# Three of four MLP passes: when the weights of the way down are loaded

## The chip, the core and the metric

The kernel runs on one core of a Trainium2 chip. The core's engines work side by side, each on its own queue of instructions in order: TensorE (PE in the profile) multiplies matrices into PSUM, VectorE (DVE) and ScalarE (ACT) work on elements, GpSimd (POOL) does some of the sums here, and SyncE (SP) issues nearly all DMAs. The metric is the device time of one execution in microseconds; lower is better.

## The reference

One layer of a decoder trunk on 1024 tokens of width 1024, all in float32: a gated linear attention with its residual, then an MLP with its residual, then a last RMSNorm. The change concerns the MLP alone:

```python
def sqrelu_mlp(h, w1, w2):
    return jnp.square(jax.nn.relu(h @ w1)) @ w2
...
        x = x + mixers[i % N_MIXERS](rms_norm(x, norm_mix), *mix_params)
        x = x + sqrelu_mlp(rms_norm(x, norm_ffn), w1, w2)
    return rms_norm(x, final_norm)
```

`w1` is 1024 x 4096 and `w2` is 4096 x 1024.

## The kernel before

**Products.** A 1024 x 1024 x 1024 product is cut into blocks of 512 ("11", "12", "21", "22") and done in seven steps by a Winograd scheme instead of eight. `form` (L147) says for each side which block or which sum of blocks a step uses; a temporary "t" holds sums. In each step the 512-blocks are multiplied by `step` (L232): four lanes of 128 rows by four k-tiles by three matmuls (`mm3`, L72), since each float32 operand is split into a rounded high part and a rest (`split`, L79: the high part on ScalarE, L81, the rest on VectorE, L82). So a step is 48 matmuls of 128 x 512. The order of the steps is 0, 5, 1, 2, 3, 4, 6 on the way up and 0 to 6 on the way down.

**Passes.** The hidden width of 4096 is handled in four chunks of 1024. The plan (L1104 to L1108) is a list: entry 0 is the attention's output product; then for each chunk c an up pass (entry 1 + 2c: `w1` columns times x, into `hd[c]`, with square and ReLU) and a down pass (entry 2 + 2c: `hd[c]` times `w2` rows, added onto y). `chunks_of` (L262) walks the plan. At step `at` it takes the operands that are ready, may load weights for the next entry, makes the operands of the next step (`operand`, L266: sums, then splits), and emits the matmuls of this step.

**The x side.** The up pass of chunk 0 makes its seven forms of x on VectorE and ScalarE (`xside`) and stores each one, split, to DRAM (`xw`, 1 MB in each of two halves). The up passes of chunks 1 to 3 have the side `Stored` (L1024): no sums and no splits, only two 1 MB loads from `xw` a step (L1034), into tiles "big". There are 8 such tiles, four to a step's operands, so a form's load waits until TensorE has finished the step before last of its use.

**The weight side.** `weight_side` (L214) loads blocks into tiles "wa" (6) and "wb" (4) in two halves of 0.5 MB. The tags (L211) cross over: the up pass has 11 and 21 in "wa", 22 and 12 in "wb"; the down pass has 11 and 21 in "wb", 12 and 22 in "wa"; both have "t" in "wa". So the loads for a down pass take the buffers of the up pass before it as these come free. The sums of the weight side run on POOL (L184), except in the up pass of chunk 0, where VectorE does them. The first two sums of a down pass are t = 12 - 11 and 12 = 22 - 12, each in two halves: four POOL operations.

**What sets the order.** TensorE's order is written by hand (`manual_schedule`). The other engines' order is laid out by the tile framework's planner at compile time: of the instructions whose inputs and buffers it reckons ready, the one earliest in the program goes first. It may so put a load several steps ahead of where the program names it. `order_after(..., wait=False)` (L41) adds an edge that only the planner obeys: this instruction is placed behind that one. At run time each queue is served in order, and a DMA whose buffer is not free holds up all that SyncE has behind it.

**The place of the change.** In `chunks_of` the weights of the next entry are loaded at `at == 5` (for a down pass 11, 12 and 22: six loads) and at `at == 6` (21: two loads). Where the present entry has stored x (entries 3, 5, 7), these loads come behind `operand(*nxt)` in the program, and in `from_down` (L924) each carries an edge to `last["xw"]`, the latest load of a stored form. At `at == 5` that is the last form of the pass. Other edges to `last["xw"]` (L980, L992, L1056) belong to the turning of x in DRAM, and stay.

Of the kernel before, what the change touches and what calls it, by code (L numbers as in the profile page):

```python
# [40 lines left out]
def order_after(tc, inst, other, wait=True):  # L41

    kind = mybir.DependencyClass.Sync if wait else mybir.DependencyClass.NoSync
    tc.add_manual_dep(inst.ins, other.ins.name, mybir.DependencyInfo(kind, mybir.DependencyReason.DATA),
                      reason="order of phases")
# [3 lines left out]
def hybrid_trunk(ctx: ExitStack, tc: tile.TileContext, x, xT, w_head, w_r, w_gk, w_up,  # L49
                 w_out, w_ff1, w_ff2, vecs, g_fin, out):  # L50
    nc = tc.nc
# [25 lines left out]
    last = {}  # L77
# [41 lines left out]
    def run(general):  # L119
# [8 lines left out]
        def half(hf):  # L128
            return slice(hf * 512, hf * 512 + 512)
# [102 lines left out]
        def step(n, lhs, rhs, sink, by_lane=False, between={}, fine=False):  # L232

            b = BANK[n]

            def product(lane, kp):
                kh, k = kp // 2, kp % 2
                if n in (0, 1, 5) and kp == 0:
                    bank[b, lane] = new("gl" if b == "U" or lane == 0 else "mm")
                ls = slice(lane * P, lane * P + P)  # L240
                mm3(bank[b, lane], lhs[kh][:, k, 0, ls], lhs[kh][:, k, 1, ls], rhs[kh][:, k, 0, :], rhs[kh][:, k, 1, :],
                    n in (0, 1, 5) and kp == 0, n in (3, 5, 6) and kp == 3, True)
                if kp == 3:
                    sink(n, lane, bank[b, lane])

            if by_lane:
                for lane in range(4):
                    for kp in range(4):
                        product(lane, kp)
                        for f in between.get((lane, kp), ()):  # L250
                            f()
            elif fine:
                for kp in range(4):
                    for lane in range(4):
                        product(lane, kp)
            else:
                for kh in range(2):
                    for lane in range(4):
                        product(lane, 2 * kh)
                        product(lane, 2 * kh + 1)  # L260

        def chunks_of(plan, ops, hooks, sinks, last_by_lane=False, turns={}):  # L262

            def operand(i, at):  # L266

                which, order = plan[i][2], plan[i][4]
                w, x_ = plan[i][which], plan[i][1 - which]
                made = {}  # L270
                for turn in turns.get((i, at), ("W", "n", "x", "X") if which == 0 else ("x", "X", "W", "n")):
                    if callable(turn):
                        turn()
                    elif turn == "x":
                        x_.sums(order[at])
                    elif turn == "X":
                        made[1 - which] = x_.split(order[at])
                    elif turn == "w":
                        w.sums(order[at])
                    elif turn == "W":  # L280
                        made[which] = w.split(order[at])
                    elif at + 1 < len(order):
                        w.sums(order[at + 1])
                return made[0], made[1]

            def load(i, names):
                if i < len(plan):
                    w = plan[i][plan[i][2]]
                    for name in names[w.s_form]:
                        w.load(name)  # L290

            if not ops:
                ops.append(operand(0, 0))
            for i, (_, _, _, sink, order) in enumerate(plan):
                for at, n in enumerate(order):
                    for f in hooks.get((i, at), ()):
                        f()
                    cur = ops.pop(0)
                    stored = getattr(plan[i][1], "stored", False)
                    loads = {5: {True: ("11", "12"), False: ("11", "12", "22")}, 6: {True: ("21", "22"), False: ("21",)}}.get(at)  # L300
                    if loads and not stored:
                        load(i + 1, loads)
                    nxt = (i, at + 1) if at + 1 < len(order) else (i + 1, 0)
                    if nxt[0] < len(plan):
                        ops.append(operand(*nxt))
                    if loads and stored:
                        load(i + 1, loads)
                    for f in hooks.get((i, at, "then"), ()):
                        f()
                    here = {k[2:]: v for k, v in hooks.items() if len(k) == 4 and k[:2] == (i, at)}  # L310
                    final_step = last_by_lane and (i, at) == (len(plan) - 1, 6)
                    step(n, *cur, sinks.get((i, at), sink), bool(here) or final_step, here, (i, at) in fine_steps)
# [176 lines left out]
        class KeptX:  # L489

            s_form = False
# [358 lines left out]
        if not general:  # L850
# [10 lines left out]
                          (2, 0, 3, 3): (g(prep_fast, 2, 1),), (2, 3, "then"): (g(prep_fast, 3, 1),),  # L861
                          (2, 4, 2, 1): (g(operands, 0, "mm"),)})
        chunks_of([(wqk, xq, 0, qk_into, PLAIN), (xk, wv, 1, v_into, PLAIN), (xr_, wR, 1, r_into, R_FIRST)], ops_a, hooks, {},
                  turns={(0, 1): ("X", split_gate, "W"), (0, 2): ("x", "X", "w", "W", lambda: last.update(sums=last["split"], s1=last["sum"], s1_low=last["low"]), "n"),
                         (0, 3): ("W", "x", "X", "n"), (2, 3): ("x", "X", "W", g(wR.sums, 3))})
# [58 lines left out]
        def from_down(c):  # L924
            def bring(a, b, kh, dst):
                f0 = 8 * c + 4 * a + 2 * kh
                load = nc.sync.dma_start(dst.rearrange("p (k n) -> p k n", k=2),
                                         w_ff2[f0:f0 + 2, :, half(b)].rearrange("k p n -> p k n"))
                if c:
                    order_after(tc, load, last["xw"], wait=False)  # L930
            return bring


# [84 lines left out]
        xw = [[dram.tile([P, 2048], F32, name=f"xw{n}{kh}{int(general)}") for kh in range(2)] for n in range(7)]  # L1018
# [3 lines left out]
                nc.sync.dma_start(xw[n][kh], tiles[kh].rearrange("p k l t -> p (k l t)").bitcast(F32))  # L1022

        class Stored:  # L1024
            s_form, stored = False, True

            def sums(self, n):
                pass
# [75 lines left out]
        plan = [(wo, so, 0, onto_x1T, PLAIN)]  # L1104
# [12 lines left out]
        for k in range(KT):  # L1117
            for i, at, f in ((2 * NC - 6, 6 + 2 * k, (turn_load, k)), (2 * NC - 6, 7 + 2 * k, (turn_blocks, k)),
                             (2 * NC - 6, 8 + 2 * k, (turn_store, k, 0)), (2 * NC - 6, 9 + 2 * k, (turn_store, k, 2)),
                             (2 * NC - 2, 5 + k, (x1_load, k)), (2 * NC - 2, 7 + k, (x1_onto, k))):  # L1120
                hooks.setdefault((i + at // 7, at % 7, "then"), []).append(g(*f))
        chunks_of(plan, ops, hooks, {}, last_by_lane=True,
                  turns={(0, at): ("x", "X", "W", "n") if at == 1 else ("W", "x", "X", "n") for at in range(1, 7)})

    flag = sb.tile([P, 1], I32, name="flag")
    with tc.manual_schedule(engines={mybir.EngineType.PE}):
        run(False)
# [3 lines left out]
    with tc.If(go_general > 0):  # L1131

        level_mask = {}
        masks = new("at").bitcast(BF16)
        pool.memset(masks, 1.0)
        for n, s in enumerate(LEVELS):
            nb = 64 // s
            m = masks[:, n * 64:(n + 1) * 64].unsqueeze(1)
            mv = m.rearrange("p o (b t) -> p (o b) t", t=s)
            pool.affine_select(mv, mv, [[-2 * s, nb], [0, s]], ALU.is_ge, 0.0, base=0, channel_multiplier=1)  # L1140
            pool.affine_select(mv, mv, [[2 * s, nb], [0, s]], ALU.is_ge, 0.0, base=s - 1, channel_multiplier=-1)
            level_mask[s] = m
        run(True)
# [50 lines left out]
```

## Time and profile before

| what | value |
|---|---|
| median of 3 runs | 1020.68 us (1020.12 to 1022.73) |
| the profiled execution's own time | 1021.63 us |
| its span in the trace | 1019.6 us, mean granted clock 0.987 |
| DMA traffic | 193.64 MB, mean 190 GB/s |

By the chain of work the passes lie so in the span: up passes of chunks 1, 2 and 3 end near 606, 767 and 927 us, that of chunk 0 near 453 us. Most of this kernel's instructions are recorded under a helper's line (L70, L81, L82, L184), so the tile names tell them apart: "big<-wa" or "big<-wb" is a split of weights, "big<-hq" one of hidden values, "wa<-" at L184 a sum of the weight side, "raw<-" or "hq<-" at L184 a sum of the hidden side, "big<-xw" a load of a stored form, "in_w_ff" the MLP's weights. L920 loads weights for a way up, L927 for a way down, L1004 to L1008 evict PSUM in an up pass.

### The profile page before, as it was taken

What the parts mean: (1) busy time and instruction counts of PE and PEld (TensorE: products, weight loads), DVE (VectorE), ACT (ScalarE), POOL (GpSimd) and SP (SyncE); (2) the same over time, 40 slices, a digit from 0 to 9 for tenths busy, and PEclk for the clock granted to TensorE, in tenths of its full rate; (3) what the DMA queues carried; (4) which work ended last, traced back from release to release, by engine and by line L of the source; (5) the groups of instructions that cost most, each with busy time, mean ns of one, the idle gap of its engine ahead of it and who ended that gap; (6) DMA issues with size and microseconds to landing.
All of it is one profiled execution on the core that took longest, in us unless ns stands there. A gap on an engine that the chain in (4) does not pass through costs nothing.

```text
span 1019.6 us, 12233 instructions
## 1 busy us (share of the span) xinstructions
PE 991.6 (97%) x4508; PEld 825.0 (81%) x4508; DVE 765.7 (75%) x899; ACT 563.6 (55%) x858; POOL 231.8 (23%) x142
## 2 busy tenths in 40 slices
PE   9999999999999999999999979999998999998996
PEld 7888878889988888888888867888886888886884
DVE  6994886868899999688544279954369976559976
ACT  7776555787784566486425362432454433664455
POOL 0000110013430000404044045032124243106360
PEclk9999999999999999999999999999998999998998
DMA  9899694666391376641247682396681216672004
GB/s 277 311 339 363 261 310 174 232 228 201 117 313 27 128 266 256 260 162 42 83 167 225 214 281 42 78 261 210 230 313 44 83 52 265 240 281 91 1 1 168
DMA packets 135692, 193.64 MB, mean 190 GB/s; under 512 B 39240, under 2 KB 100808, under 8 KB 124104
## 3 DMA queue, kind: packets, MB, share of 16 engines
q1 hardware_dynamic: 135064, 192.37, 54.8%
q8 instruction: 37, 0.61, 0.2%
q10 hardware_dynamic: 560, 0.40, 0.1%
q14 instruction: 31, 0.25, 0.1%
HBM read 146.62 MB, written 46.14 MB: 189 GB/s over the span
## 4 chain that ended last, share of the span: by engine, by line
PE 77%; DVE 6%; ACT 2%; issue 1%; DVEq 0%; ACTq 0%
PE gl L70 51%; PE mm L70 25%; DVE big L82 2%; DVE raw L184 1%; DVE hq L184 1%; DVE vx L1078 0%; PE mm L638 0%; ACT g L698 0%; PE mm L717 0%; ACT big L81 0%; ACT wb L81 0%; DVE big L785 0%; PE gl L717 0%; DVE g L1098 0%; DVE g L707 0%
## 5 line engine op out<-in xcount | busy, mean ns | idle before, releaser
L70 PE MATMUL gl<-big,big 128*128 128x512 f32 x2712 | 636.8, 392 | 16.0 <-ACT hq L1008 9.2
L70 PEld LDWEIGHTS gl<-big,big 128*128 128x128 f32 x2712 | 513.1, 190 | 125.1 <-ACT hq L1008 10.0
L70 PE MATMUL mm<-big,big 128*128 128x512 f32 x1224 | 288.7, 389 | 0.0
L70 PEld LDWEIGHTS mm<-big,big 128*128 128x128 f32 x1224 | 229.7, 188 | 48.1 <-ACT g L812 0.4
L82 DVE TENSOR_TENSOR big<-wa,big 128x1024 fp32r<-128x1024 f32 (+1 forms) x118 | 154.8, 1333 | 90.3 <-ACT big L81 90.2
L81 ACT ACTIVATE big<-wa 128x1024 fp32r<-128x1024 f32 (+1 forms) x118 | 118.7, 1039 | 106.3 <-PE gl L70 58.6
L184 POOL TENSOR_TENSOR wa<-wa,wb 128x1024 f32<-128x1024 f32 x14 | 44.5, 3184 | 350.4 <-DVE big L82 190.0
L184 POOL TENSOR_TENSOR wa<-wa,wa 128x1024 f32<-128x1024 f32 x28 | 82.6, 2959 | 103.8 <-DVE big L82 103.1
L82 DVE TENSOR_TENSOR big<-hq,big 128x1024 fp32r<-128x1024 f32 x48 | 65.9, 1381 | 33.1 <-ACT big L81 33.0
L82 DVE TENSOR_TENSOR big<-wb,big 128x1024 fp32r<-128x1024 f32 x50 | 71.2, 1442 | 26.0 <-ACT big L81 25.9
L81 ACT ACTIVATE big<-wb 128x1024 fp32r<-128x1024 f32 x50 | 51.1, 1053 | 57.6 <-PE gl L70 26.6
L81 ACT ACTIVATE big<-raw 128x1024 fp32r<-128x1024 f32 x42 | 43.6, 1056 | 67.3 <-DVE raw L184 44.5
L81 ACT ACTIVATE big<-hq 128x1024 fp32r<-128x1024 f32 x48 | 48.8, 1052 | 41.7 <-PE gl L70 21.5
L82 DVE TENSOR_TENSOR big<-raw,big 128x1024 fp32r<-128x1024 f32 x42 | 64.7, 1559 | 4.6 <-ACT big L81 4.6
L184 POOL TENSOR_TENSOR wa<-wb,wa 128x1024 f32<-128x1024 f32 x14 | 41.0, 2943 | 37.3 <-DVE big L82 37.3
L558 POOL COPY top<-g 128x4 f32<-128x4 f32 x8 | 7.2, 896 | 182.0 <-DVE g L550 182.0
L1013 ACT ACTIVATE hq<-hq 128x1024 f32<-128x1024 f32 x24 | 25.4, 1057 | 38.4 <-DVE hq L1006 38.4
L1004 ACT ACTIVATE hq<-gl 128x512 f32<-128x512 f32 x36 | 21.4, 595 | 36.4 <-PE gl L70 36.3
L680 POOL TENSOR_SCALAR g<-g,est 128x256 f32<-128x256 f32 x28 | 29.1, 1056 | 52.0 <-DVE g L677 33.0
L1051 DVE TENSOR_TENSOR vx<-gl,vx 128x512 f32<-128x512 f32 x44 | 29.1, 680 | 8.8 <-PE gl L70 8.7
L70 PE MATMUL gl<-wb,wa 128*128 128x256 f32 x180 | 32.1, 310 | 0.0
L70 PEld LDWEIGHTS gl<-wb,wa 128*128 128x128 f32 x180 | 26.3, 190 | 2.0
(201 smaller groups left out, 890.0 us busy)
## 6 DMA issues: line engine op xcount, KB each, us to landing
big<-xw SPq DMA_DIRECT2D x42, 1024.0 KB, 6.8
big<-xv SPq DMA_DIRECT2D x20, 1024.0 KB, 6.2
xv<-big SPq DMA_DIRECT2D x14, 1024.0 KB, 7.5
xw<-big SPq DMA_DIRECT2D x14, 1024.0 KB, 4.6
wa<-in_w_ff SPq DMA_DIRECT2D x32, 256.0 KB, 4.1
wb<-in_w_ff SPq DMA_DIRECT2D x32, 256.0 KB, 3.6
wa<-in_w_ff SPq DMA_DIRECT2D x16, 512.0 KB, 10.2
wb<-in_w_ff SPq DMA_DIRECT2D x16, 512.0 KB, 8.6
```

Of the source, the lines that this page charges most:

```text
L70: pe.matmul(o, w, m, start=start, stop=stop, skip_group_check=partial)
L81: last["split"] = act.activation(hi, src, AF.Copy)
L82: last["low"] = dve.tensor_tensor(lo, src, f32(hi), op=ALU.subtract)
L184: op = self.eng.tensor_tensor(*(self.ap(b, kp, 2) for b in (o, x_, y_)), op=op)
L558: pool.tensor_copy(top[:, 8 * h + 4 * hf:8 * h + 4 * hf + 4].unsqueeze(2), a[:, :, P - 1:P])
L680: pool.tensor_scalar(S[:, vs], Z[:, vs], g, None, op0=ALU.mult)
L1004: act.activation(d, p_, AF.Copy)
L1013: act.activation(d2, d2, AF.Relu)
L1051: dve.tensor_tensor(yd, p_, yd, op=ALU.add)
```

## The change

The branch for stored x goes, and with it the edge in `from_down`: in every pass the weights of the next entry come ahead of the next operands in the program, and the planner is free to place them.

```diff
@@ -296,15 +296,13 @@
                     cur = ops.pop(0)
-                    stored = getattr(plan[i][1], "stored", False)
-                    loads = {5: {True: ("11", "12"), False: ("11", "12", "22")}, 6: {True: ("21", "22"), False: ("21",)}}.get(at)
-                    if loads and not stored:
-                        load(i + 1, loads)
+                    if at == 5:
+                        load(i + 1, {True: ("11", "12"), False: ("11", "12", "22")})
+                    if at == 6:
+                        load(i + 1, {True: ("21", "22"), False: ("21",)})
                     nxt = (i, at + 1) if at + 1 < len(order) else (i + 1, 0)
                     if nxt[0] < len(plan):
                         ops.append(operand(*nxt))
-                    if loads and stored:
-                        load(i + 1, loads)
@@ -924,10 +922,8 @@
                 f0 = 8 * c + 4 * a + 2 * kh
-                load = nc.sync.dma_start(dst.rearrange("p (k n) -> p k n", k=2),
-                                         w_ff2[f0:f0 + 2, :, half(b)].rearrange("k p n -> p k n"))
-                if c:
-                    order_after(tc, load, last["xw"], wait=False)
+                nc.sync.dma_start(dst.rearrange("p (k n) -> p k n", k=2),
+                                  w_ff2[f0:f0 + 2, :, half(b)].rearrange("k p n -> p k n"))
@@ -1022,7 +1018,7 @@
         class Stored:
-            s_form, stored = False, True
+            s_form = False
```

For entries 1, 2, 4, 6 and 8 the program's order is what it was; entries 3, 5 and 7 are concerned.

## The prediction

> **What bounds the kernel now.** I read the page first, then the chain of work that ended last, then the timeline wherever that chain leaves TensorE, and last the SyncE queue's own timeline. From the page:
>
> ```profile
> span 1019.6 us, 12233 instructions
> PE 991.6 (97%) x4508; PEld 825.0 (81%) x4508; DVE 765.7 (75%) x899; ACT 563.6 (55%) x858; POOL 231.8 (23%) x142
> L70 PE MATMUL gl<-big,big 128*128 128x512 f32 x2712 | 636.8, 392 | 16.0 <-ACT hq L1008 9.2
> ```
>
> TensorE is busy for 991.6 of 1019.6 us, so only its gaps and its clock can be worth anything. The group that holds most of the matmuls has 16.0 us of idle time in all. The timeline shows where they lie (start, duration, engine and line, then in brackets the idle time before it and its releaser):
>
> ```profile
> 612.65 14.28 PE L70 MATMUL gl<-big,big 128*128 128x512 f32 x53 [6.53 <-DVE big L82]
> 772.95 13.18 PE L70 MATMUL gl<-big,big 128*128 128x512 f32 x48 [4.59 <-ACT hq L1008]
> 932.14 13.77 PE L70 MATMUL gl<-big,big 128*128 128x512 f32 x48 [4.57 <-ACT hq L1008]
> ```
>
> 6.53 + 4.59 + 4.57 = 15.69 us: nearly all of it is three gaps, each at the place where an up pass with stored forms of x (plan entries 3, 5 and 7) hands over to its way down (entries 4, 6, 8). The work after each gap is slow as well. The chain shows an undisturbed step, and the view by stretches shows the clock behind the first gap (columns: stretch, length, busy time and count of PE, PEld, DVE, ACT, POOL, granted clock, DMA share, GB/s):
>
> ```profile
> 745.25 10.89 PE gl L70 x48
> 610.00:615.00 5.00, 2.35 (x6) 1.87 (x7) 4.93 (x6) 3.47 (x4) 0.00 (x0) 0.50 0.00 0
> ```
>
> A step of 48 matmuls takes 10.89 us, 0.227 us each. At that pace the three pieces above would take 12.02, 10.89 and 10.89 us; they took 14.28, 13.18 and 13.77, which is 2.26 + 2.29 + 2.88 = 7.43 us more. The granted clock was 0.50 right behind the first gap. So a gap costs its length and a restart at a low clock: 15.69 + 7.43 = 23.1 us in all, about 7.7 us a pass.
>
> What makes a gap? The first one, in the timeline:
>
> ```profile
> 584.17 0.99 SPq L1034 DMA_DIRECT2D big<-xw  x2
> 586.42 3.17 SPq L927 DMA_DIRECT2D wa<-in_w_ff  x4
> 595.66 1.22 DVE L184 TENSOR_TENSOR raw<-hq,hq 128x1024 f32<-128x1024 f32 x1
> 596.42 6.07 POOL L184 TENSOR_TENSOR wa<-wa,wb 128x1024 f32<-128x1024 f32 x2 [41.89 <-DMA wa<-in_w_ff]
> 596.79 3.43 DVE L82 TENSOR_TENSOR big<-hq,big 128x1024 fp32r<-128x1024 f32 x1
> 602.46 6.66 POOL L184 TENSOR_TENSOR wa<-wa,wa 128x1024 f32<-128x1024 f32 x2
> 606.84 3.36 DVE L184 TENSOR_TENSOR raw<-hq,hq 128x1024 f32<-128x1024 f32 x1
> 610.23 1.23 DVE L184 TENSOR_TENSOR hq<-hq,hq 128x1024 f32<-128x1024 f32 x1
> 611.37 2.36 DVE L82 TENSOR_TENSOR big<-wb,big 128x1024 fp32r<-128x1024 f32 x2
> ```
>
> SyncE issues the last form of x at 584.17, when TensorE gives its buffers back, and the down weights only behind it. They land at 596.42, POOL's idle time (41.89 us) ends there, and its four weight sums fill the time to 609.1. Through just that time VectorE's operations with two SBUF inputs take about 3.4 us; before it and after it the same operations take 1.22. VectorE is then the late one: its splits give TensorE the first operands of the way down at 612.65. In the other two passes the same slowing reaches TensorE another way: ScalarE waits in its queue for a slowed sum, and the evictions that free the PSUM banks stand behind that wait.
>
> ```profile
> 756.77 1.22 DVE L184 TENSOR_TENSOR raw<-hq,hq 128x1024 f32<-128x1024 f32 x1
> 763.58 6.66 POOL L184 TENSOR_TENSOR wa<-wa,wa 128x1024 f32<-128x1024 f32 x2
> 771.36 1.06 ACT L81 ACTIVATE big<-raw 128x1024 fp32r<-128x1024 f32 x1 [8.69 <-DVE raw L184]
> ```
>
> **The control is in the same trace.** The first up pass (entry 1) makes its forms of x instead of loading them, and its down weights are not held back already. Its SyncE issues, its POOL sums, and the stretch over its hand-over:
>
> ```profile
> 387.51 1.52 SPq L927 DMA_DIRECT2D wa<-in_w_ff  x2
> 400.18 2.11 SPq L927 DMA_DIRECT2D wb<-in_w_ff  x2
> 407.59 1.53 SPq L927 DMA_DIRECT2D wa<-in_w_ff  x2
> 417.94 3.31 POOL L184 TENSOR_TENSOR wa<-wa,wb 128x1024 f32<-128x1024 f32 x1 [121.06 <-DVE big L82]
> 427.15 3.25 POOL L184 TENSOR_TENSOR wa<-wa,wa 128x1024 f32<-128x1024 f32 x1
> 431.00:453.00 22.00, 22.00 (x99) 18.22 (x98) 19.79 (x22) 17.62 (x20) 0.00 (x0) 1.00 0.54 199
> ```
>
> The weights were issued as buffers came free, two to four steps ahead of the place where the program names them; POOL did its four sums from 417.94 to 430.4; in the 22 us up to the hand-over POOL is idle and TensorE busy for 22.00.
>
> **The change part by part.** No instruction is added, none is dropped, no byte moves that did not move before. For three passes it (a) lets six 0.5 MB loads go ahead of the two 1 MB loads of the last form, (b) drops the planner's edge to that form, so that they can go up as soon as their buffers are free, and (c) sets the two loads of block 21 ahead of the next operands, which on SyncE changes nothing that is needed soon (21 enters at the sixth step down): I cost (c) at nothing.
>
> *When buffers come free.* In the pass of the first gap:
>
> ```profile
> 537.66 5.66 POOL L184 TENSOR_TENSOR wa<-wa,wa 128x1024 f32<-128x1024 f32 x2 [14.71 <-DVE big L82]
> 540.65 0.79 SPq L1034 DMA_DIRECT2D big<-xw  x2
> 552.12 2.41 POOL L184 TENSOR_TENSOR wa<-wb,wa 128x1024 f32<-128x1024 f32 x1 [1.17 <-DVE big L82]
> 562.41 0.81 SPq L1034 DMA_DIRECT2D big<-xw  x2
> 573.58 1.23 DVE L82 TENSOR_TENSOR big<-wa,big 128x1024 fp32r<-128x1024 f32 x1 [0.20 <-ACT big L81]
> 573.40:584.30 10.90, 10.90 (x50) 9.03 (x49) 4.09 (x5) 2.73 (x5) 0.00 (x0) 1.00 0.67 218
> ```
>
> and from the page's part on DMA issues (count, size, median us to landing):
>
> ```profile
> wa<-in_w_ff SPq DMA_DIRECT2D x16, 512.0 KB, 10.2
> ```
>
> The sum that frees the buffers of the up block 11 ends at 543.3, the one that frees those of 12 at 554.5, and the up block 21 is split by 574.8. So the loads can be out by about 576, and landed by 587 at the latest, taking the 10.2 us that such a load needed behind other traffic. If the third load takes the buffers of the temporary sums, as the control suggests, POOL starts at about 573.4 and, at the 12.7 us it needed at the hand-over, is done by 586, nine before the hand-over. VectorE has 4.09 us of work in those 10.9 us, so slowed operations find room there.
>
> *What is late next.* Without POOL beside it, VectorE's eight operations from 595.66 take 8 x 1.22 = 9.8 us: done at 605.4. TensorE's own last step ends at 612.65 - 6.53 = 606.1. That fits by 0.7 us, and the control shows the same hand-over fitting. In the other passes five operations from 756.77 end at 762.9, while TensorE ran to 768.4.
>
> *The sum.* All three gaps and their restarts go: 1021.63 us, the profiled execution's own time (its span of 1019.6 and 2.0 around it), less 23.1 is 998.5. That execution lies 0.95 us above the median of the runs, 1020.68; from the median it is 997.6. I take **998.0**. There is no more to win: TensorE's other 12 us without work (1019.6 - 991.6 - 15.7) are not at these places.
>
> [...]
>
> *The loads of x, now behind weights.* They are all that can lose. These rows bound it (the first is the page's, the second the view of the tile's loads, the third SyncE's waits):
>
> ```profile
> big<-xw SPq DMA_DIRECT2D x42, 1024.0 KB, 6.8
> DMA to landing us min/median/max: 4.7/6.8/7.7
> SPq L927 <- DVE wa L184: 14.1, 4, 7.5
> ```
>
> A form is issued as a step begins and needed one step later, 10.9 us. With 0.4 us to issue and 6.8 to land, 3.7 us are spare. One block of weights ahead of it (1 MB; x's two loads move 2 MB in about 6.8, so at most 3.4 us) fits just. Below nothing there is no cost. From above: if SyncE holds a weight load at its head for w us while its buffer is still in use, the form is late by about w + 3.4 - 3.7. By the rows of POOL and SyncE, w would be 543.3 - 540.65 = 2.7 us at worst for the buffers of the up block 11, if the planner sets that load ahead of the form: 2.4 us of gap. For the control's loads the longest such wait was 7.5 us. I take nothing, since the end of POOL's sums and the return of x's buffers lie within 3 us of each other and a late second half is needed only half a step later; I keep both ends.
>
> **The rivals.**
>
> *Contention only moves.* POOL's sums still cost VectorE 2.2 us for each two-input operation beside them. If one such operation in each pass is one that TensorE waits for, 3 x 2.2 = 6.6 us are given back: about 1005. For it: the 3.4 us rows. Against: the control's sums ran beside splits and TensorE did not pause; VectorE is lightly loaded there. [...] Chance 0.09.
>
> *Block 22 stays late.* If its load comes only behind the last form, two of POOL's four sums (6.66 us) stay at the hand-over and slow two operations by 2.2 us each. Of the 4.4 us, 0.7 is spare, so a gap of 3.7 and a restart of 2.5 stay in each pass, 18.6 in all; 4.5 are won: about 1016. Against: 21 is split a whole step before x's buffers come back. Chance 0.07.
>
> *The change does not do what it says.* The planner places the loads where they are: 1020.7. Against: the control's place is up to four steps earlier. Chance 0.05.
>
> *Slower: SyncE is held at its head.* A weight load set ahead of a form of x waits for its buffer, and the form stands behind it. Price by the longest wait in the control: 7.5 + 3.4 - 3.7 = 7.2 us of gap plus a restart of 2.5 = 9.7 a pass, against 7.7 won: 2.0 x 3 = 6 us slower, about 1027. It decides from w = 5.5 us on. For it: the queue is served in order, and the control's loads did wait. Against: the rows above give 2.7. Chance 0.07.
>
> **How the numbers follow.** Forecast 998.0 with 0.72. About 3 us, 0.3%, is what a measurement of this kernel can tell from no change. Faster by more: 0.72 + 0.09 + 0.07 = 0.88; within: 0.05; slower: 0.07. The range takes in the forecast and the moved contention (0.81): from 996, the sum with the lowest of the runs and one us for its own error, to 1006.
>
> **What would show it.** Right: POOL's sums in plan entries 3, 5, 7 about two steps before the hand-over, no DMA wait before them; VectorE's operations behind the last form at 1.22 us; no gap of TensorE there, its clock 1.00. Wrong: a gap in the middle of an up pass whose releaser is a load of xw; SyncE waits at line 927 of over 5 us; or operations of 3.4 us still at the hand-over. A time over 1006 would mean that one of these holds.

## The result and the profile after

| | before | after |
|---|---|---|
| median of four runs | 1020.78 us | 998.30 us (998.02 to 999.30) |
| ratio of the runs | | 0.9778, 95% interval 0.9761 to 0.9795 |
| span of the profiled execution | 1019.6 us | 996.3 us |

The change makes the kernel 22.5 us faster; 998.0 was forecast. First the page's lines that answer to those of before:

```profile
span 996.3 us, 12235 instructions
PE 983.6 (99%) x4508; PEld 819.8 (82%) x4508; DVE 748.7 (75%) x899; ACT 563.8 (57%) x858; POOL 229.9 (23%) x142
L70 PE MATMUL gl<-big,big 128*128 128x512 f32 x2712 | 629.3, 389 | 0.7 <-DVE big L82 0.4
```

The same 2712 matmuls are busy for 629.3 us instead of 636.8, and their idle time fell from 16.0 us to 0.7. That is 7.5 + 15.3 = 22.8 of the 23.3 us by which the span shrank: the restarts at a low clock (0.50 in the first 4 us behind each of the three gaps of the kernel before) and the gaps. The view by stretches (length, busy time and count of PE, PEld, DVE, ACT, POOL, granted clock, DMA share, GB/s) covers the three hand-overs; the second and third now come sooner in the span:

```profile
595.00:612.70 17.70, 17.70 (x80) 14.66 (x79) 17.63 (x16) 15.78 (x21) 1.54 (x2) 1.00 0.48 117
744.00:762.00 18.00, 18.00 (x82) 14.88 (x81) 16.16 (x16) 15.86 (x20) 4.17 (x3) 1.00 0.60 213
898.00:916.00 18.00, 18.00 (x81) 14.92 (x80) 17.51 (x16) 14.44 (x19) 2.32 (x1) 1.00 0.08 34
```

TensorE is busy throughout and its clock is 1.00. And the timeline of the first of these passes:

```profile
540.84 2.73 SPq L925 DMA_DIRECT2D wa<-in_w_ff  x2
543.67 0.89 SPq L1030 DMA_DIRECT2D big<-xw  x2
575.68 5.54 SPq L925 DMA_DIRECT2D wb<-in_w_ff  x2
581.31 0.93 SPq L925 DMA_DIRECT2D wa<-in_w_ff  x2
585.02 5.74 POOL L184 TENSOR_TENSOR wa<-wa,wb 128x1024 f32<-128x1024 f32 x2 [30.63 <-DVE hq L1002]
590.72 5.77 POOL L184 TENSOR_TENSOR wa<-wa,wa 128x1024 f32<-128x1024 f32 x2
595.51 2.06 DVE L184 TENSOR_TENSOR raw<-hq,hq 128x1024 f32<-128x1024 f32 x1
597.60 1.23 DVE L184 TENSOR_TENSOR hq<-hq,hq 128x1024 f32<-128x1024 f32 x1
```

The weights go up in three parts, blocks 12, 11 and 22, all before the last form at 584. POOL's four sums end at 596.5, one us into the hand-over: VectorE's first operation there takes 2.06 us, the next 1.23. Two splits of weights just ahead of it were slowed too (1.72 us at 586.79 and 3.16 us at 588.68, against 1.22 in the second pass), but TensorE did not pause for them. In the other two passes the sums run from 738.3 to 747.8 and from 874.7 to 885.1, before their hand-overs.

### The profile page after: what moved, and what is told of

It reads as the page before. It is cut to its first block, busy times and chain, and to the rows that moved or that the text cites. A ratio compares the mean times of both kernels' runs of the same rounds, so it can differ in the third digit from the quotient of the medians.

```text
span 996.3 us, 12235 instructions
## 1 busy us (share of the span) xinstructions
PE 983.6 (99%) x4508; PEld 819.8 (82%) x4508; DVE 748.7 (75%) x899; ACT 563.8 (57%) x858; POOL 229.9 (23%) x142
## 4 chain that ended last, share of the span: by engine, by line
PE 81%; DVE 2%; ACT 1%; issue 1%; DVEq 0%; ACTq 0%
PE gl L70 55%; PE mm L70 26%; DVE vx L1074 0%; PE mm L636 0%; ACT g L696 0%; PE mm L715 0%; DVE big L82 0%; ACT wb L81 0%; DVE big L783 0%; PE gl L715 0%; DVE g L1094 0%; DVE g L705 0%; DVE g L675 0%; ACT hq L717 0%; ACT big L725 0%
## 5 line engine op out<-in xcount | busy, mean ns | idle before, releaser
L70 PE MATMUL gl<-big,big 128*128 128x512 f32 x2712 | 629.3, 389 | 0.7 <-DVE big L82 0.4
L184 POOL TENSOR_TENSOR wa<-wa,wb 128x1024 f32<-128x1024 f32 x14 | 42.1, 3018 | 298.8 <-DVE big L82 205.9
L184 POOL TENSOR_TENSOR wa<-wa,wa 128x1024 f32<-128x1024 f32 x28 | 80.0, 2868 | 133.7 <-DVE big L82 133.1
L82 DVE TENSOR_TENSOR big<-wb,big 128x1024 fp32r<-128x1024 f32 x50 | 64.8, 1314 | 25.5 <-ACT big L81 25.5
L82 DVE TENSOR_TENSOR big<-hq,big 128x1024 fp32r<-128x1024 f32 x48 | 61.6, 1292 | 26.5 <-ACT big L81 26.5
L82 DVE TENSOR_TENSOR big<-raw,big 128x1024 fp32r<-128x1024 f32 x42 | 67.7, 1631 | 4.9 <-ACT big L81 4.9
L556 POOL COPY top<-g 128x4 f32<-128x4 f32 x8 | 10.1, 1266 | 180.5 <-DVE g L548 180.5
L1002 DVE TENSOR_TENSOR hq<-gl,hq 128x512 f32<-128x512 f32 x24 | 16.0, 686 | 19.6 <-PE gl L70 19.6
```

Source lines behind the costliest of these rows:

```text
L70: pe.matmul(o, w, m, start=start, stop=stop, skip_group_check=partial)
L82: last["low"] = dve.tensor_tensor(lo, src, f32(hi), op=ALU.subtract)
L184: op = self.eng.tensor_tensor(*(self.ap(b, kp, 2) for b in (o, x_, y_)), op=op)
L556: pool.tensor_copy(top[:, 8 * h + 4 * hf:8 * h + 4 * hf + 4].unsqueeze(2), a[:, :, P - 1:P])
L1002: dve.tensor_tensor(d, p_, d, op=ALU.add)
```

## The experiments

Theory A says that the gaps are VectorE slowed by POOL's sums beside it; theory B, that they are the late weights themselves. The first two runs part the two: late weights without sums at the hand-over, and early weights with them.

**Late loads, sums held back.** The kernel before, in which the first sums of each of the three ways down wait for the split of block 11.

```diff
 # Side.sums
+                        if n == 1 and getattr(self, "held", None):
+                            order_after(tc, op, last[self.held])
 # plan
+            down = weight_side(False, from_down(c), pool)
+            down.held = "low" if c else None
```

> Loads late as before, but POOL's first sums of the way down (t = 12 - 11) wait for VectorE's split of down block 11. Theory A (the gap is VectorE slowed by POOL's sums beside it): VectorE's operations at the hand-over take 1.22 us again although the weights land as late as before; the gaps of 6.5, 4.6 and 4.6 us at the hand-overs go or shrink under 1.5 us each; the sums now run some 10 us later, and may cost 1 to 3 us a pass there: 998 to 1010 us. Theory B (the gap is the weights' late landing itself): gaps as before, 1018 to 1024 us.

Measured: 1012.9 us, ratio 0.9914 (0.9897 to 0.9932). The timeline at the first hand-over:

```profile
600.61 1.22 DVE L184 TENSOR_TENSOR raw<-hq,hq 128x1024 f32<-128x1024 f32 x1
603.00 2.36 DVE L82 TENSOR_TENSOR big<-wb,big 128x1024 fp32r<-128x1024 f32 x2
605.44 6.66 POOL L184 TENSOR_TENSOR wa<-wa,wb 128x1024 f32<-128x1024 f32 x2 [50.50 <-DVE big L82]
606.52 3.32 DVE L184 TENSOR_TENSOR raw<-raw,hq 128x1024 f32<-128x1024 f32 x1
619.89 1.43 PE L70 MATMUL gl<-big,big 128*128 128x512 f32 x5 [2.49 <-DVE big L82]
```

The weights are issued as late as before (blocks 12 and 22 from 586.81, against 586.42), yet VectorE works at 1.22 us until 605.4, and TensorE goes over without a gap. As soon as POOL starts, VectorE's next operation takes 3.32 us. The stall is moved: TensorE waits 2.49 us one step later, and again at other steps down; the large group of matmuls idles 10.7 us in all (in the profiled execution, at 1016.4 us the longest of the four). The hand-over answers to A. The time lies outside what A was given: 14.6 us above the changed kernel, 4.9 a pass, where I allowed 1 to 3. That the contention cost this is shown at the first wait alone. At the later waits (2.42, 1.90 and 2.77 us) POOL is idle and VectorE is the releaser and busy almost without a pause (for 3.00, 4.93 and 4.89 us of the 3, 5 and 5 us around them), so that VectorE is still in arrears there is likely but not shown.

**Early loads, sums at the hand-over.** The changed kernel, in which those sums wait for the last eviction of the sixth step up (`last["evict"]`, set at that eviction).

```diff
+            down = weight_side(False, from_down(c), pool)
+            down.held = "evict" if c else None
```

> Loads early as in the changed kernel, but POOL's first sums of the way down wait for VectorE's last eviction of the sixth step up, so that they run at the hand-over as before. Theory A: operations of 3.4 us and gaps of 4 to 6.5 us with a low clock behind them come back in all three passes: 1014 to 1022 us. Theory B: the weights are in place, so no gaps: 997 to 1001 us.

Measured: 1020.7 us, ratio 0.9989 (0.9978 to 1.0). The timeline, the first two lines at the first hand-over and then TensorE behind all three:

```profile
595.46 6.62 POOL L184 TENSOR_TENSOR wa<-wa,wb 128x1024 f32<-128x1024 f32 x2 [41.34 <-DVE hq L1004]
599.74 3.43 DVE L184 TENSOR_TENSOR raw<-hq,hq 128x1024 f32<-128x1024 f32 x1
612.14 13.92 PE L70 MATMUL gl<-big,big 128*128 128x512 f32 x53 [6.44 <-DVE big L82]
770.49 14.92 PE L70 MATMUL gl<-big,big 128*128 128x512 f32 x53 [4.13 <-DVE big L82]
931.42 13.54 PE L70 MATMUL gl<-big,big 128*128 128x512 f32 x48 [4.57 <-ACT hq L1006]
```

The weights are there, and the whole gain is gone: gaps of 6.44, 4.13 and 4.57 us against 6.53, 4.59 and 4.57 before. Theory B falls.

**Late loads, sums on VectorE.** The kernel before, with the three ways down's sums taken from POOL.

```diff
-weight_side(False, from_down(c), pool), 1,
+weight_side(False, from_down(c), dve if c else pool), 1,
```

> Loads late as before, but the three ways down have their weight sums on VectorE instead of POOL. Theory A (POOL beside VectorE makes the gap): no operation of 3.4 us at the hand-over; VectorE has up to four more operations of 1.22 us there (4.9 us), of which 0.7 is spare, so gaps of 0 to 4 us a pass: 1000 to 1015 us. Rival (what counts is when the weights land, or VectorE's load): gaps of 4.5 us or more, 1018 us and up.

Measured: 999.4 us, ratio 0.9783 (0.9762 to 0.9804), which no run here tells from the change's own. The page's line of engines, and the timeline of the first hand-over:

```profile
PE 984.3 (99%) x4508; PEld 820.4 (82%) x4508; DVE 744.1 (75%) x923; ACT 562.9 (56%) x858; POOL 157.1 (16%) x118
```

```profile
600.86 1.22 DVE L184 TENSOR_TENSOR raw<-hq,hq 128x1024 f32<-128x1024 f32 x1
603.25 2.35 DVE L82 TENSOR_TENSOR big<-wb,big 128x1024 fp32r<-128x1024 f32 x2
606.66 2.35 DVE L184 TENSOR_TENSOR wa<-wa,wb 128x1024 f32<-128x1024 f32 x2
```

The loads stay behind the last form, and TensorE's large group idles 0.8 us. VectorE does 24 operations more (923 against 899) and is busy for 21.6 us less than before (744.1 against 765.7). A sum that takes POOL 2.4 to 3.4 us takes VectorE 1.18 (2.35 for two).

**Both remedies.** The same edit on the changed kernel.

> Both remedies at once: loads early as in the changed kernel, and the weight sums of the three ways down on VectorE. Theory A (there is one cause, and each remedy alone removes it): no gain over the changed kernel or over the run with late loads and sums on VectorE, 997 to 1000 us, TensorE's idle time in the large group under 1 us. Rival (each removes a part of its own): 990 to 996 us.

Measured: 998.7 us, ratio 0.9769 (0.9751 to 0.9787); idle time of the large group 0.4 us. The two do not add: one cause, which either removes.

**The edge alone.** Only the planner's edge goes.

```diff
-                if c:
-                    order_after(tc, load, last["xw"], wait=False)
```

> Only the planner's edge to the last form goes; the loads stay behind the next operands in the program. Theory A with the buffers deciding the place: the planner hoists the loads as in the changed kernel, since their buffers come free before those of the last form: 997 to 1001 us, no gaps. Rival (the program's order does it): loads stay behind the last form, 1018 to 1024 us.

Measured: 1011.9 us, ratio 0.9902 (0.9872 to 0.9933), between the two. In the second of the three passes the planner put only block 11 ahead of the last form, and the rest behind it:

```profile
744.49 0.81 SPq L1032 DMA_DIRECT2D big<-xw  x2
745.35 2.48 SPq L927 DMA_DIRECT2D wa<-in_w_ff  x4
754.22 5.99 POOL L184 TENSOR_TENSOR wa<-wa,wb 128x1024 f32<-128x1024 f32 x2 [33.95 <-DMA wa<-in_w_ff]
770.73 12.68 PE L70 MATMUL gl<-big,big 128*128 128x512 f32 x48 [3.15 <-ACT hq L1006]
```

The sums stand at the hand-over again, and so does a gap. In the first pass blocks 11 and 22 stayed behind (gap 4.70 us); in the third all three blocks went ahead, the sums ended at 898.2, and there is no gap. Free buffers do not decide the place alone; the program's order does too.

**The order alone.** The edge stays, and so points to the form before the last.

```diff
-                    if loads and not stored:
+                    if loads:
                         load(i + 1, loads)
...
-                    if loads and stored:
-                        load(i + 1, loads)
```

> Only the program's order is changed; the edge stays, and now points to the form before the last. The loads can go no earlier than about 574 in the first pass, 10 us ahead of the last form. Theory A: landed by about 585, POOL's sums from there to about 598, over the start of the hand-over: gaps of 0 to 2 us a pass, 998 to 1006 us. Rival (only a lead of two steps or more helps): 1012 to 1022 us.

Measured: 1002.9 us, ratio 0.9823 (0.9803 to 0.9843), as A had it; a lead of one step does. But there is one new gap, in the third pass. From the timeline, one of VectorE's small operations at 0.16 us ahead of POOL's sums, then the stretch of the sums, VectorE's evictions and TensorE:

```profile
879.64 0.16 DVE L114 SCALAR_TENSOR_TENSOR rstd<-st,rstd 128x1 f32<-128x1 f32 x1
891.09 4.76 POOL L184 TENSOR_TENSOR wa<-wa,wb 128x1024 f32<-128x1024 f32 x2 [31.67 <-DMA wa<-in_w_ff]
893.55 2.32 DVE L114 SCALAR_TENSOR_TENSOR rstd<-st,rstd 128x1 f32<-128x1 f32 x1
895.80 4.74 POOL L184 TENSOR_TENSOR wa<-wa,wa 128x1024 f32<-128x1024 f32 x2
895.90 2.31 DVE L1061 TENSOR_TENSOR ss<-rstd 128x1 f32<-128x1 f32 x1
898.25 3.37 DVE L1062 SCALAR_TENSOR_TENSOR vx<-vx,ss,g 128x1024 f32<-128x1024 f32 x1
901.54 2.47 DVE L1004 TENSOR_TENSOR hq<-gl,hq 128x512 f32<-128x512 f32 x4
902.32 23.40 PE L70 MATMUL gl<-big,big 128*128 128x512 f32 x102 [2.42 <-issue]
```

This gap is the same contention once more. The sums fell on operations of the normalisation of x that VectorE does in this pass: the same ones took 0.16, 0.16 and 1.28 us a step earlier, and take 2.32, 2.31 and 3.37 us here. The four evictions of the sixth step stand behind them, and the last step up adds onto the PSUM banks that they read out: the first of them ends at 902.22, and TensorE goes on at 902.32. The last form of x stands behind six weight loads and takes longer than the median of 6.8 us before; the view of the tile's loads gives the time to landing of its two halves:

```profile
889.05 0.81 SPq L1032 DMA_DIRECT2D big<-xw  x2
DMA to landing us min/median/max: 8.4/9.5/10.5
```

That does not explain the gap: both halves had landed by 900.0, 2.3 us before TensorE went on, and in the second pass of the changed kernel the two halves of the last form took 8.3 and 10.5 us without any gap. TensorE's releaser is recorded only as "issue", so that it waited for the eviction is read from the times and the program; no run moved the sums off these operations alone.

**The forms late, twice and three times loaded.** The changed kernel, with the first half of the last form loaded k times into the same tile, which is the price of the rival that ended on the slower side.

```diff
-                    last["xw"] = nc.sync.dma_start(w.bitcast(F32), xw[n][kh])
+                    for _ in range(2 if n == 6 and kh == 0 else 1):
+                        last["xw"] = nc.sync.dma_start(w.bitcast(F32), xw[n][kh])
```

> The changed kernel, but in each of the three passes the first half of the last form of x is loaded twice into the same tile, so that the second load waits on SyncE for the first to land: the form comes about 6 us (one landing) late, and SyncE is held as long. The prediction's price (a spare of 3.7 us, both halves needed at the step's start): gaps of about 2.5 us a pass, 1004 to 1012 us. Rival (the second half is needed only half a step later, spare of 5 to 6 us): gaps of 0 to 1 us, 998 to 1002 us.

Measured: 1014.8 us, ratio 0.9937 (0.9916 to 0.9959).

> The same with three loads of that half: about 12 us late. The prediction's price: gaps of 8 to 9 us and a restart of 2.5 us a pass, more than the 7.7 us that the change wins: 1026 to 1034 us, slower than the kernel before. Rival (spare of 5 to 6 us): gaps of 6 us and restarts: 1018 to 1026 us, about where the kernel before is. If forms of x had far more spare than either says, 998 to 1005 us.

Measured: 1033.6 us, ratio 1.0118 (1.0095 to 1.014). SyncE's issues of the last form in the first pass and TensorE behind it, of the run with two loads and then of that with three:

```profile
583.50 8.70 SPq L1031 DMA_DIRECT2D big<-xw  x3
597.26 25.01 PE L70 MATMUL gl<-big,big 128*128 128x512 f32 x102 [2.91 <-ACT hq L1010]
```

```profile
597.97 0.32 SPq L1031 DMA_DIRECT2D big<-xw  x1
603.07 25.57 PE L70 MATMUL gl<-big,big 128*128 128x512 f32 x102 [8.00 <-DMA big<-xw]
```

With two, the last of the three issues ends at 592.2, so the first half is issued about 8.4 us late for a gap of 2.91: 5.5 us were spare. With three it is 13.8 us late (597.97 against 584.2) for a gap of 8.00: 5.8 us spare. The other passes, counted from the start of the step in which the form is issued, give 5.8 and 5.8 with two, 3.9 and 6.0 with three; in the one with 3.9 the last load of that half took 6.9 us to land, in the others 4.8 to 5.2.

With two loads neither price held. The gaps (2.91, 2.56 and 2.30 us) were near the 2.5 us of the prediction's price by luck: the half came 8.4 us late and not 6, and the spare was 5.5 us and not 3.7. The time is 2.8 us above that price's bound. In the profiled execution, at 1012.46 us the shortest of the four, the gaps and restarts (25.01 against 23.1 us for 102 matmuls at full pace, about the same in each pass) make 13.3 us of the 14.4 by which it is longer than the changed kernel's; what the longer executions have on top is not shown. With three the time is within the prediction's bounds and above the rival's, by the same luck: 13.8 us late and not 12.

## Why the prediction was right, point by point

- **The sum.** Gaps and restarts were read as 15.69 + 7.43 us from three rows. 15.3 and 7.5 went. This step stands to 0.4 us, and it was nearly the whole size of the result (22.8 of 23.3 us of the span).
- **The cause.** That VectorE is slowed by the sums, and not only fed late, was argued from 3.4 against 1.22 us. It is now shown: by the run with early weights and sums at the hand-over, which lost everything, and by the run with late weights and no sums on POOL, which won everything. For the clean hand-over VectorE's eight operations were put at 9.8 us; in the run with the sums held back they took 9.3, from 596.07 to 603.00 + 2.36 = 605.36.
- **Where the sums would go.** This step failed. "POOL starts at about 573.4 and ... is done by 586": in that pass, the first, the sums started at 585.0 and ended at 596.5, not nine us ahead of the hand-over but one us into it. In the second the sums ended just as the hand-over began, at 747.8; only in the third did they end a step ahead, at 885.1. I had taken a free buffer for an issue. Block 11's buffers were free at about 554, but the planner put its load at 575.68, behind two more forms. It cost nothing, as only one operation of the hand-over was hit, and that by 0.8 us: this was luck and not foreseen. In the edge-only run, where blocks stayed behind the last form in two passes, the large group idles 8.2 us.
- **The loads of x.** "The form is late by about w + 3.4 - 3.7" was too high. In the first pass SyncE held a weight load at its head until 543.67, 3.0 us past the form's time before, which was foreseen as 2.7; by the bound that made 2.4 us of gap, and there was none. The spare of 3.7 us was mis-sized: measured, 5.5 to 6.0 us in five of six cases. The step needs the first half alone to begin, and that lands in 4.8 to 5.2 us in these five, where 6.8 was taken. That a late second half does no harm is shown by the changed kernel's first pass: the last form's second half, issued at 584.4, took 11.0 us to land, until 595.4, while its step had begun at 594.7 (one step of 10.89 us behind 583.82, the start of the stretch below) and TensorE did not pause. The value that I took, nothing, was right. TensorE's row and the view of that load's landing:

```profile
583.82 34.16 PE L70 MATMUL gl<-big,big 128*128 128x512 f32 x150
DMA to landing us min/median/max: 11.0/11.0/11.0
```

- **The rivals.** *Contention only moves*: not here, but real; moved later instead of earlier it gave back 14.6 of the 22.5 us (1012.9 against 998.3). *Block 22 stays late*: no run left block 22 alone behind. The edge alone left 12 and 22 behind in the second pass, all four sums stood at the hand-over, and the gap was 3.15 us; the rival reckoned 3.7 for two sums. *SyncE held at its head*: its point was put at w = 5.5 us, which is a form late by 5.5 + 3.4 = 8.9 us. That was somewhat early. A form late by 8.4 us leaves the kernel 6.5 us faster than before, one by 13.8 us makes it 12.3 us slower; on a straight line between the two the point lies at about 10.3 us (an estimate).

How the two engines slow each other can be read from durations. In the run with early loads and the sums at the hand-over, where both worked on two SBUF inputs, each got through one operation in 3.3 to 3.4 us (6.62 for two on POOL, 3.43 on VectorE). That is near the sum of their times without the other, 2.39 us (4.78 for two on POOL, with only VectorE's evictions of 0.69 us beside them) and 1.18 us (2.35 for two on VectorE, with the sums taken from POOL): 3.57. And in the run with the order alone a VectorE operation that took 0.16 us a step earlier took 2.32 beside POOL's sums, about as long as one whole sum. The row for POOL, from the changed kernel's second pass:

```profile
743.03 4.78 POOL L184 TENSOR_TENSOR wa<-wa,wa 128x1024 f32<-128x1024 f32 x2
```

What makes the two hold each other up so is not shown by any run.

## What to carry to other kernels

A stall at a hand-over whose releaser is one engine can be made by another that waits for nothing, as POOL's sums made the gap of 6.53 us that VectorE released: compare the duration of the same operation inside and outside the stall before looking for a late input. Work given to POOL was not free for VectorE here, where both read two SBUF inputs (1.22 us became 3.43); place it where VectorE has room, or leave it on VectorE, which here took less time in all (744.1 us busy against 765.7). Even VectorE's smallest operations count: one of 0.16 us took 2.32 beside a sum, and a row of them held up an eviction that, by the times, TensorE was waiting for. How far a planner hoists a load follows from the program's order and the edges together, so read the queue that comes out.

## What was not expected of the hardware

The clock fell after one gap of TensorE and not after a longer one. In the run with late loads and the sums held back a gap of 1.90 us is followed by a clock of 0.50 for some three us (802.7 to 805.7); in the run with the order alone the clock stays at 1.00 behind a gap of 2.42 us. TensorE's row and the stretches of the first, then two stretches of the second:

```profile
801.76 1.79 PE L70 MATMUL gl<-big,big 128*128 128x512 f32 x5 [1.90 <-DVE big L82]
802.70:803.70 1.00, 1.00 (x4) 0.80 (x3) 1.00 (x2) 1.00 (x2) 0.00 (x0) 0.50 0.58 173
804.70:805.70 1.00, 1.00 (x4) 0.81 (x3) 1.00 (x2) 0.00 (x0) 0.00 (x0) 0.50 0.81 224
806.70:807.70 1.00, 1.00 (x6) 0.82 (x5) 1.00 (x3) 0.00 (x0) 0.00 (x0) 1.00 0.16 49
```

```profile
902.30:904.00 1.70, 1.68 (x7) 1.41 (x8) 1.70 (x3) 1.15 (x2) 0.00 (x0) 1.00 0.64 223
904.00:906.00 2.00, 2.00 (x10) 1.66 (x9) 1.12 (x2) 2.00 (x3) 0.00 (x0) 1.00 0.00 0
```

The length of the gap alone does not decide it in these two; what does was not tried.
